# Bidirectional delta-net and attention encoder layer: small products of the block inversion issued in turn over different squares of the TensorE array

## Chip, cores, metric

One core of one Trainium2 chip. The metric is the device time of one execution in microseconds. An encoder layer runs on a prompt of 1024 tokens and a sample of 256 tokens.

## What is computed

A projection of the input feeds two groups of heads, a gated delta rule that runs forward and backward, and differential attention. Their outputs are projected, and a SwiGLU layer follows. The part that matters here is the delta rule. Each chunk of tokens needs the inverse of a unit triangular matrix, which the reference gets by a triangular solve:

```
decay = exp(where(incl, gc[..., :, None] - gc[..., None, :], -inf))
m = where(strict, einsum('bhnid,bhnjd->bhnij', kb, k) * decay, 0.0)
a_mat = m + eye(CHUNK)
rhs = concatenate([v * beta[..., None], kb * exp(gc)[..., None]], -1)
sol = triangular_solve(a_mat, rhs, left_side=True, lower=True, unit_diagonal=True)
u, w = sol[..., :DV], sol[..., DV:]
```

## The kernel before, in words

The kernel has phases. Phase A (`phase_a`) makes the dense projections on TensorE (line 172, tiles `dps`) and, between them, everything that the delta rule needs ahead of its scan: convolution and transposes, Gram products (line 430, `kq_ps`), decays, and the inverses. Attention scores (lines 839 and 840, `s_ps`), the scan with its loads `ld` (line 973), the output projection and the SwiGLU layer (lines 1281 and 1507) follow.

Five sets of eight 128x128 matrices per direction are inverted. VectorE inverts the 32x32 diagonal blocks (`invert_blocks`). They go out to HBM in plain and transposed form and come back into the tiles `UD` (`spread_blocks`: stores at lines 512 and 514, eight loads at line 517, issued by SP). `k.UD[0]`, which the listings call UD_772, holds the plain form; `k.UD[1]`, UD_773, the transposed one. Then `invert_levels` joins blocks on TensorE, in four stages with a `yield` between them; u counts the eight matrices and d the two directions:

- stage 1: 32 matmuls of 32x32 from `N` and UD_773 into one PSUM tile `inv_ps`, copied by VectorE to `Z`;
- stage 2: 48 matmuls of 32x32 from `Z` and `UD`, in six groups of eight, copied to `UD` by ScalarE and VectorE in turn;
- stage 3: per direction 8 matmuls of 64x64, each with its own `inv_ps`, copied to `Z` by ScalarE;
- stage 4: 16 matmuls of 64x64 in two groups, copied to `UD`, which is then stored for the scan (line 578).

The pool of `inv_ps` has one buffer. Every matmul reads 32 or 64 partitions (a group of rows of the array) and writes 32 or 64 (a group of columns); the pair is called a square here. The helper `pe` issues the eight matmuls of one group, all on one square:

```
for u in range(8):
    lhs, rhs = fn(u)
    nc.tensor.matmul(ps[rows, c0 + u * m:c0 + (u + 1) * m], lhsT=lhs, rhs=rhs, start=True, stop=True)
```

The stages stand in generators that `advance()` steps between pieces of the dense projection, and a scheduler then orders the instructions of each engine by its own estimate of when their inputs are there. So a change in one helper can move instructions on all queues.

Of the kernel before, what the change touches and what calls it, by code (L numbers as in the profile page):

```python
# [519 lines left out]
def diag(k, t, b, d=None):  # L520

    r = slice(32 * b, 32 * b + 32)
    return k.UD[t][r, :, r] if d is None else k.UD[t][r, 8 * d:8 * d + 8, r]


def invert_levels(k, si, vh, N, G):

    nc, V, A, PO = k.nc, k.nc.vector, k.nc.scalar, k.nc.gpsimd
    q = [slice(32 * b, 32 * b + 32) for b in range(4)]
    lo, up = slice(0, 64), slice(64, 128)  # L530
    UD = [[t[:, 8 * d:8 * d + 8] for t in k.UD] for d in range(2)]

    def pe(ps, rows, c0, m, fn):
        for u in range(8):
            lhs, rhs = fn(u)
            nc.tensor.matmul(ps[rows, c0 + u * m:c0 + (u + 1) * m], lhsT=lhs, rhs=rhs, start=True, stop=True)
        return ps[rows, c0:c0 + 8 * m].rearrange("p (u c) -> p u c", u=8)

    Z = k.gi.tile([P, 2, 8, 64], F32, tag="Z", name="Z")
    ps = k.pi.tile([P, 512], F32, tag="inv", name="inv_ps")  # L540
    for x, y in ((0, 1), (2, 3)):
        for d in range(2):
            pe(ps, q[y], 256 * d, 32, lambda u: (N[d][q[x], u, q[y]], diag(k, 1, x, d)[:, u]))
    for y in (1, 3):
        V.tensor_copy(Z[q[y], :, :, 0:32], ps[q[y], :].rearrange("p (d u c) -> p d u c", d=2, u=8))
    yield
    ps = k.pi.tile([P, 512], F32, tag="inv", name="inv_ps")
    out = []
    for d in range(2):
        U, D = UD[d]  # L550
        for x, y in ((0, 1), (2, 3)):
            if d == 0 or x == 2:
                r = pe(ps, q[x], 256 * d, 32, lambda u: (Z[q[y], d, u, 0:32], diag(k, 0, y, d)[:, u]))
                out.append((U[q[x], :, q[y]], r))
            if d == 1 or x == 0:
                r = pe(ps, q[y], 256 * d, 32, lambda u: (diag(k, 0, y, d)[:, u], Z[q[y], d, u, 0:32]))
                out.append((D[q[y], :, q[x]], r))
    for i, (o, r) in enumerate(out):
        (V.tensor_copy if i % 2 else A.copy)(o, r)
    yield  # L560
    for d in range(2):
        U, D = UD[d]
        ps = k.pi.tile([P, 512], F32, tag="inv", name="inv_ps")
        r = pe(ps, up, 0, 64, lambda u: (N[d][lo, u, up], D[lo, u, lo]))
        A.copy(Z[up, d], r)
    yield
    ps = k.pi.tile([P, 512], F32, tag="inv", name="inv_ps")
    U, D = UD[0]
    r0 = pe(ps, lo, 0, 64, lambda u: (Z[up, 0, u, :], U[up, u, up]))
    Ub, Db = UD[1]  # L570
    r1 = pe(ps, up, 0, 64, lambda u: (Ub[up, u, up], Z[up, 1, u, :]))
    A.copy(U[lo, :, up], r0)
    A.copy(Db[up, :, lo], r1)
    off = 4 * NT[si] + (vh * 8 if si == 1 else 0)
    V.tensor_tensor(out=Db, in0=Db, in1=G.nbeta[:, off:off + 8].unsqueeze(2).to_broadcast([P, 8, P]), op=ALU.mult)
    for g in range(2):
        for d, res in ((0, U), (1, Db)):
            nc.sync.dma_start(out=k.S.rec[si][vh][g][:, :, 6 * d, :], in_=res[:, 4 * g:4 * g + 4, :])
    yield
# [12 lines left out]
def phase_a(k):  # L592
    nc, tc = k.nc, k.tc
    with ExitStack() as es:
# [63 lines left out]
        def prep(si, vh, c3):  # L658
            N = []
            flag = Ctx()  # L660
            flag.done = False

            def front():
                yield from prep_front(k, si, vh, c3, k.G[si], N, flag, lambda: k.gp2 and len(blocks_) + len(levels) < 2)

            def invert():
                yield from invert_blocks(k, si, vh)

            def back():
                spread_blocks(k, si, vh)  # L670
                yield from invert_levels(k, si, vh, N, k.G[si])

            fronts.append(([front()], [invert(), back()]))
            return flag
# [989 lines left out]
```

## Time and profile before

| what | us |
|---|---|
| timed, median of 3 | 1756.84 |
| timed, lowest and highest | 1756.25 and 1760.42 |
| the profiled execution | 1751.05 |
| its span, first to last instruction | 1749.3 |

In the profile PE is TensorE's matmuls, PEld its weight loads, DVE VectorE, ACT ScalarE, POOL GpSimd, and SP the queue that issues most DMAs. An fp32 matmul appears as two weight loads and two matmul records, so the 32 matmuls of a stage are x64. Where a helper issues many matmuls all have the helper's line, 536 before and 538 in the changed kernel. The granted clock is 1.00 for 2.4 GHz and 0.50 for 1.2 GHz. Numbers in brackets behind a row are idle time of its engine ahead of it, and what ended that.

### The profile page before, as it was taken

To read this page: it belongs to the slowest core of one execution; us is meant where nothing else is said; L and a number is where in the kernel's file an instruction comes from. 1 tells how busy PE (TensorE), PEld (TensorE's weight loads), DVE (VectorE), ACT (ScalarE), POOL (GpSimd) and SP (SyncE) were. 2 spreads that over 40 slices of the span, in tenths; PEclk is the share of its full clock that TensorE was granted. 3 is DMA by queue.
4 is the path that set the end of the run, shared out by engine and by line. 5 is a ranking of instruction groups with operands and counts; after the bars stand their busy time and mean duration, and the time that the engine had idled before them with its cause. 6 is when DMAs were issued, how large, how long until landed. Compare 5 with 4: busy or idle time off the path is not lost.

```text
span 1749.3 us, 27337 instructions
## 1 busy us (share of the span) xinstructions
PE 1694.2 (97%) x10234; PEld 1471.2 (84%) x10234; DVE 1191.9 (68%) x2114; ACT 777.5 (44%) x1518; POOL 213.1 (12%) x197
## 2 busy tenths in 40 slices
PE   8999999999988999999999999999999999999998
PEld 8898888888867998788888888888888887888886
DVE  4635968878575589885676866556656665666696
ACT  4457486564337677775114322222222223543330
POOL 1000000000014445532330000000000000000011
PEclk9999999999988999999999999999999999999999
DMA  6234265676667996516521544333333524975541
GB/s 219 65 100 115 75 164 176 155 207 168 184 172 218 280 266 200 173 51 223 159 96 43 191 149 149 111 128 131 116 136 125 175 99 138 391 254 172 174 158 72
DMA packets 253554, 279.02 MB, mean 160 GB/s; under 512 B 47713, under 2 KB 198127, under 8 KB 252015
## 3 DMA queue, kind: packets, MB, share of 16 engines
q1 hardware_dynamic: 243519, 265.19, 48.5%
q10 hardware_dynamic: 9904, 12.10, 2.0%
q8 instruction: 80, 1.31, 0.3%
q14 instruction: 51, 0.42, 0.1%
HBM read 183.80 MB, written 93.43 MB: 158 GB/s over the span
## 4 chain that ended last, share of the span: by engine, by line
PE 54%; DMA 1%; ACT 1%; DVE 1%; issue 1%; POOLq 0%; POOL 0%; DVEq 0%; SPq 0%; ACTq 0%
PE dn_ps L1507 15%; PE gy_ps L1281 9%; PE gs_ps L1281 7%; PE gx_ps L1281 6%; PE gz_ps L1281 6%; PE om_ps L172 6%; PE gp_ps L1281 3%; DMA worw<-in_w_out_dram 1%; PE o_ps L879 1%; PE x_ps L1186 0%; ACT ap L843 0%; PE s_ps L839 0%; ACT woh L1166 0%; PE s_ps L840 0%; PE tt_ps L866 0%
## 5 line engine op out<-in xcount | busy, mean ns | idle before, releaser
L1297 ACT CAST sph<-wraw 128x512 fp32r<-128x512 f32 x92 | 57.0, 623 | 195.4 <-PE gy_ps L1281 124.4
L315 POOL TENSOR_TENSOR rs_r<-lva,mhalf 128x1 f32<-128x1 f32 x20 | 29.5, 1475 | 835.5 <-DVE lva L1143 817.1
L172 PE MATMUL dps<-xh,whi 128*128 128x512 f32 (+1 forms) x552 | 126.1, 363 | 0.0
L172 PE MATMUL dps<-xh,wlo 128*128 128x512 f32 (+1 forms) x552 | 124.5, 360 | 0.0
L172 PE MATMUL dps<-xl,whi 128*128 128x512 f32 (+1 forms) x552 | 123.4, 363 | 0.0
L1297 ACT CAST sph<-wsum 128x512 fp32r<-128x512 f32 x80 | 49.8, 622 | 156.6 <-PE gy_ps L1281 48.8
L1507 PE MATMUL dn_ps<-tth,ssh 128*128 128x512 f32 x280 | 108.9, 389 | 0.0
L1507 PE MATMUL dn_ps<-ttl,ssh 128*128 128x512 f32 x280 | 108.8, 389 | 0.0
L1507 PE MATMUL dn_ps<-tth,ssl 128*128 128x512 f32 x280 | 108.1, 389 | 0.0
L172 PEld LDWEIGHTS dps<-xh,wlo 128*128 128x128 f32 x552 | 94.8, 191 | 14.8
L172 PEld LDWEIGHTS dps<-xl,whi 128*128 128x128 f32 x552 | 94.2, 193 | 15.4
L172 PEld LDWEIGHTS dps<-xh,whi 128*128 128x128 f32 x552 | 94.5, 191 | 14.6
L841 DVE TENSOR_REDUCE ast<-s_ps 128x1 f32<-128x1024 f32 (+1 forms) x80 | 83.5, 1056 | 21.7 <-PE s_ps L840 19.6
L1298 DVE TENSOR_TENSOR spl<-wraw,sph 128x512 fp32r<-128x512 f32 x92 | 63.0, 687 | 48.2 <-PE gs_ps L1281 29.9
L334 DVE SCALAR_TENSOR_TENSOR c<-pad,cw,c 128x1024 f32<-128x1024 f32 (+1 forms) x96 | 82.1, 884 | 17.1 <-ACT c L332 16.6
L843 ACT ACTIVATE ap<-s_ps,ast 128x1024 f32<-128x1024 f32 (+1 forms) x80 | 80.0, 1001 | 29.4 <-DVE ast L841 29.1
L1298 DVE TENSOR_TENSOR spl<-wsum,sph 128x512 fp32r<-128x512 f32 x80 | 55.0, 688 | 46.6 <-issue 20.4
L1498 ACT CAST ssh<-sraw 128x640 fp32r<-128x640 f32 x77 | 56.0, 727 | 47.6 <-PE dn_ps L1507 34.3
L1499 DVE TENSOR_TENSOR ssl<-sraw,ssh 128x640 fp32r<-128x640 f32 x77 | 63.1, 820 | 16.8 <-ACT ssh L1498 13.1
L839 PE MATMUL s_ps<-akl,aq 128*128 128x512 f32 (+1 forms) x144 | 63.7, 444 | 7.7 <-ACT ap L843 7.6
L855 POOL TENSOR_TENSOR ap<-ap,ap 128x512 f32<-128x512 f32 (+2 forms) x60 | 63.0, 1069 | 64.6 <-ACT ap L852 31.6
L879 PE MATMUL o_ps<-av,tt 128*128 128x128 f32 x544 | 64.2, 275 | 0.0
(398 smaller groups left out, 4258.9 us busy)
## 6 DMA issues: line engine op xcount, KB each, us to landing
ld<-rec SPq DMA_DIRECT2D x160, 192.0 KB, 4.2
sraw<-hs SPq DMA_DIRECT2D x77, 320.0 KB, 4.3
wraw<-in_w_gate_up_dram SPq DMA_DIRECT2D x22, 1024.0 KB, 5.7
wraw<-in_w_in_dram SPq DMA_DIRECT2D x26, 512.0 KB, 4.5
wdraw<-in_w_down_dram SPq DMA_DIRECT2D x11, 1024.0 KB, 5.1
ws<-wdraw SPq DMA_DIRECT2D x11, 1024.0 KB, 3.9
traw<-ws SPq DMA_DIRECT2D x44, 256.0 KB, 4.5
araw<-dqk SPq DMA_DIRECT2D x40, 256.0 KB, 5.4
```

Of the source, the lines that this page charges most:

```text
L172: nc.tensor.matmul(out, lhsT=a(i), rhs=b(i), start=start and j == 0, stop=stop and j == len(seq) - 1)
L334: V.scalar_tensor_tensor(out=out, in0=pad[:, so + w:so + w + n], scalar=k.cw[:, w * 12 + ti:w * 12 + ti + 1], in1=out, op0=ALU.mult, op1=A ...
L839: nc.tensor.matmul(ps[:, o:o + w], lhsT=a.q[m][:, qs], rhs=a.kl[m][:, k0 + o:k0 + o + w], start=True, stop=False)
L841: V.tensor_reduce(out=st[:, m:m + 1], in_=ps, op=ALU.max, axis=AX.X, negate=True)
L843: A.activation(p, ps, AF.Exp, bias=st[:, m:m + 1], accum_out=a.s0[:, i:i + 1] if m == 0 else st[:, 2:3])
L855: nc.gpsimd.tensor_tensor(out=pr[0][:, c], in0=pr[0][:, c], in1=pr[1][:, c], op=ALU.add)
L879: nc.tensor.matmul(ps[:, j * P:(j + 1) * P], lhsT=tt[:, i, j * P:(j + 1) * P], rhs=a.v[:, v0 + i, :], start=i == 0, stop=i == NT[a.si] - 1)
L1281: m = nc.tensor.matmul(ps, lhsT=a(i), rhs=b(i), start=start and j == 0, stop=stop and j == len(seq) - 1, skip_group_check=again)
L1297: A.copy(hi, src)
L1298: V.tensor_tensor(out=lo, in0=src, in1=f32(hi), op=ALU.subtract)
L1499: V.tensor_tensor(out=lo, in0=src, in1=f32(hi), op=ALU.subtract)
L1507: nc.tensor.matmul(ps, lhsT=a[:, c], rhs=b, start=z == 0 and j == 0, stop=z == NPR - 1 and j == 2)
```

## The change

`pe` takes several groups at once and issues, for each u, one matmul of every group before it goes to the next u. Stage 1 is issued as two such calls (one for each direction, over two squares), stage 2 as one call over its six groups on four squares, stage 4 as one call over its two groups. Stage 3 has one group per call, as before. The list of the six groups of stage 2 is written out by a helper `product`, in an order in which neighbours use different squares where they can; which of the copies behind stage 2 ScalarE and VectorE take is given by that order.

```
-    def pe(ps, rows, c0, m, fn):
+    def pe(ps, *jobs):
         for u in range(8):
-            lhs, rhs = fn(u)
-            nc.tensor.matmul(ps[rows, c0 + u * m:c0 + (u + 1) * m], lhsT=lhs, rhs=rhs, start=True, stop=True)
-        return ps[rows, c0:c0 + 8 * m].rearrange("p (u c) -> p u c", u=8)
+            for rows, c0, m, fn in jobs:
+                lhs, rhs = fn(u)
+                nc.tensor.matmul(ps[rows, c0 + u * m:c0 + (u + 1) * m], lhsT=lhs, rhs=rhs, start=True, stop=True)
+        return [ps[rows, c0:c0 + 8 * m].rearrange("p (u c) -> p u c", u=8) for rows, c0, m, fn in jobs]
...
-    for x, y in ((0, 1), (2, 3)):
-        for d in range(2):
-            pe(ps, q[y], 256 * d, 32, lambda u: (N[d][q[x], u, q[y]], diag(k, 1, x, d)[:, u]))
+    for d in range(2):
+        pe(ps, *((q[y], 256 * d, 32, lambda u, x=x, y=y: (N[d][q[x], u, q[y]], diag(k, 1, x, d)[:, u])) for x, y in ((0, 1), (2, 3))))
...
+    def product(o, x, y, d, left):
+        outs.append(o)
+        if left:
+            jobs.append((q[y], 256 * d, 32, lambda u: (diag(k, 0, y, d)[:, u], Z[q[y], d, u, 0:32])))
+        else:
+            jobs.append((q[x], 256 * d, 32, lambda u: (Z[q[y], d, u, 0:32], diag(k, 0, y, d)[:, u])))
+    (Uf, Df), (Ub, Db) = UD
+    product(Uf[q[0], :, q[1]], 0, 1, 0, False)
+    product(Uf[q[2], :, q[3]], 2, 3, 0, False)
+    product(Df[q[1], :, q[0]], 0, 1, 0, True)
+    product(Db[q[3], :, q[2]], 2, 3, 1, True)
+    product(Db[q[1], :, q[0]], 0, 1, 1, True)
+    product(Ub[q[2], :, q[3]], 2, 3, 1, False)
+    out = list(zip(outs, pe(ps, *jobs)))
...
-    r0 = pe(ps, lo, 0, 64, lambda u: (Z[up, 0, u, :], U[up, u, up]))
-    r1 = pe(ps, up, 0, 64, lambda u: (Ub[up, u, up], Z[up, 1, u, :]))
+    r0, r1 = pe(ps, (lo, 0, 64, lambda u: (Z[up, 0, u, :], U[up, u, up])), (up, 0, 64, lambda u: (Ub[up, u, up], Z[up, 1, u, :])))
```

On TensorE, stages 1 and 2 of the first inversion stood like this before (a row with UD_773 and 32x32 is stage 1, rows with Z are stage 2):

```order
L536 MATMUL inv_ps<-UD_773,N 32x32 x32
L430 MATMUL kq_ps<-kqT 128x256 x4
L397 MATMUL t_ps<-identr,raw 128x128 x4
L172 MATMUL dps<-xh_153,whi 128x512 x5
L172 MATMUL dps<-xl_218,whi 128x512 x8
L536 MATMUL inv_ps<-UD_772,Z 32x32 x8
L536 MATMUL inv_ps<-Z,UD_772 32x32 x8
L536 MATMUL inv_ps<-UD_772,Z 32x32 x8
L536 MATMUL inv_ps<-Z,UD_772 32x32 x8
L536 MATMUL inv_ps<-UD_772,Z 32x32 x8
L536 MATMUL inv_ps<-Z,UD_772 32x32 x8
```

The same place in the changed kernel, cut behind the first rows of stage 2:

```order
L538 MATMUL inv_ps<-UD_773,N 32x32
L430 MATMUL kq_ps<-kqT 128x256 x3
L538 MATMUL inv_ps<-UD_773,N 32x32 x31
L430 MATMUL kq_ps<-kqT 128x256
L397 MATMUL t_ps<-identr,raw 128x128 x4
L172 MATMUL dps<-xh_153,whi 128x512 x5
L172 MATMUL dps<-xl_218,whi 128x512 x8
L172 MATMUL dps<-xh_217,wlo 128x512 x8
L172 MATMUL dps<-xh_217,whi 128x512
L538 MATMUL inv_ps<-UD_772,Z 32x32 x2
L538 MATMUL inv_ps<-Z,UD_772 32x32 x3
L538 MATMUL inv_ps<-UD_772,Z 32x32 x3
```

Stage 1 is parted into its first matmul and the other 31, with three Gram products between them, and stage 2 stands behind nine more dense matmuls and changes square after every matmul or two.

On SP, the DMAs between the last preparations of the second inversion's blocks and its loads, before (514 stores the transposed blocks, 517 loads them, 182 loads weights of the projection):

```order
L469 DMA Wb<-nblk_68 64x1024
L517 DMA UD_772<-ublk_70 32x16x32 x4
L514 DMA ublk_70<-itmp 64x1024
L469 DMA Wb<-nblk_68 64x1024
L359 DMA rec_66<-vn 512x1x128
L404 DMA e_f<-gc_58 128x512
L517 DMA UD_773<-ublk_70 32x16x32 x4
L182 DMA wraw<-in_w_in_dram 128x8x128
```

And in the changed kernel:

```order
L512 DMA ublk_70<-Ub 64x1024
L517 DMA UD_772<-ublk_70 32x16x32 x4
L514 DMA ublk_70<-itmp 64x1024
L182 DMA wraw<-in_w_in_dram 128x8x128
L517 DMA UD_773<-ublk_70 32x16x32 x4
```

The stores and loads of `Wb`, `vn` and `e_f` have gone ahead of this piece, and a weight load (182) stands between the store of the transposed blocks and their four loads.

On TensorE, the fifth inversion's stage 1 and the attention scores between it and stage 2, before:

```order
L839 MATMUL s_ps<-akl,aq 128x512
L840 MATMUL s_ps<-akh,aq 128x512
L536 MATMUL inv_ps<-UD_773,N 32x32 x32
L839 MATMUL s_ps<-akl,aq 128x512
L840 MATMUL s_ps<-akh,aq 128x512
L839 MATMUL s_ps<-akl,aq 128x512
L840 MATMUL s_ps<-akh,aq 128x512
L536 MATMUL inv_ps<-UD_772,Z 32x32 x8
```

And in the changed kernel, whose lines from the score matmuls on stand eight further down (847 and 848 for 839 and 840):

```order
L847 MATMUL s_ps<-akl,aq 128x512
L848 MATMUL s_ps<-akh,aq 128x512
L538 MATMUL inv_ps<-UD_773,N 32x32 x32
L847 MATMUL s_ps<-akl,aq 128x512
L848 MATMUL s_ps<-akh,aq 128x512
L847 MATMUL s_ps<-akl,aq 128x512
L848 MATMUL s_ps<-akh,aq 128x512
L847 MATMUL s_ps<-akl,aq 128x512
L848 MATMUL s_ps<-akh,aq 128x512
L847 MATMUL s_ps<-akl,aq 128x512
L848 MATMUL s_ps<-akh,aq 128x512
L538 MATMUL inv_ps<-UD_772,Z 32x32 x2
```

Eight score matmuls instead of four stand between the two stages; ahead of stage 1 there are now 16 score matmuls where there were eight.

## Rows read from the trace of the kernel before

**Rows 1.** The page: busy time, share of the span and count of TensorE and the others; TensorE's busy tenths in 40 slices of the span; its granted clock in the same slices.

```profile
PE 1694.2 (97%) x10234; PEld 1471.2 (84%) x10234; DVE 1191.9 (68%) x2114; ACT 777.5 (44%) x1518; POOL 213.1 (12%) x197
...
PE   8999999999988999999999999999999999999998
...
PEclk9999999999988999999999999999999999999999
```

**Rows 2.** All engines by windows. Columns: the stretch in us, its length, then busy us and count for PE, PEld, DVE, ACT and POOL, the granted clock, DMA share and GB/s.

```profile
234.60:238.00 3.40, 3.40 (x11) 2.58 (x10) 0.42 (x1) 1.56 (x6) 0.00 (x0) 0.50 0.80 246
238.00:323.00 85.00, 85.00 (x508) 73.42 (x507) 72.61 (x124) 64.99 (x147) 3.12 (x3) 1.00 0.68 182
323.00:326.80 3.80, 2.20 (x51) 1.67 (x50) 3.80 (x8) 0.00 (x0) 0.00 (x0) 0.99 0.85 199
326.80:333.60 6.80, 6.80 (x38) 5.67 (x35) 5.38 (x16) 5.16 (x9) 3.18 (x2) 0.50 0.40 127
...
398.50:401.90 3.40, 1.92 (x35) 1.41 (x35) 3.33 (x9) 0.56 (x2) 0.00 (x0) 0.99 0.83 151
401.90:408.70 6.80, 6.80 (x56) 6.06 (x54) 6.42 (x17) 4.63 (x12) 0.00 (x0) 0.50 0.62 186
...
510.60:514.50 3.90, 0.37 (x2) 0.00 (x0) 1.85 (x2) 0.00 (x0) 0.00 (x0) 1.00 0.90 272
514.50:535.00 20.50, 17.13 (x180) 13.54 (x180) 10.43 (x16) 12.14 (x18) 5.12 (x4) 0.50 0.50 106
...
600.00:1000.00 400.00, 386.92 (x2440) 341.44 (x2439) 307.66 (x587) 212.01 (x432) 132.27 (x117) 1.00 0.51 162
1000.00:1749.00 749.00, 738.54 (x3681) 628.34 (x3679) 485.12 (x800) 229.96 (x377) 14.23 (x10) 1.00 0.45 156
```

**Rows 3.** The same view for the instructions of line 536 alone. Columns: stretch, length, PE and PEld busy with counts, clock, DMA share, GB/s. In order: stage 1, stage 2, second half of stage 3, and stage 4 of the first inversion; stages 1, 2 and 4 of the fifth.

```profile
224.13:226.17 2.04, 2.03 (x64) 2.00 (x64) 1.00 1.03 324
231.51:234.16 2.65, 2.64 (x96) 2.61 (x96) 1.00 0.56 159
...
251.60:252.66 1.06, 1.06 (x16) 1.00 (x16) 1.00 1.02 183
259.63:261.45 1.82, 1.82 (x32) 1.76 (x32) 1.00 0.04 9
...
517.02:520.35 3.33, 3.33 (x64) 3.27 (x64) 0.50 0.81 183
522.36:526.67 4.31, 4.31 (x96) 4.26 (x96) 0.50 0.40 107
539.74:541.56 1.82, 1.82 (x32) 1.76 (x32) 1.00 0.01 5
```

**Rows 4.** Order of time on PE, the first inversion's stage 2 up to and behind the first change of group. Columns: start, length, then engine, line and form; inv_ps<-UD,Z and inv_ps<-Z,UD are the two kinds of groups.

```profile
231.52 0.59 PE L536 MATMUL inv_ps<-UD,Z 32*32 32x32 f32 x13
231.92 0.21 PE L536 MATMUL inv_ps<-Z,UD 32*32 32x32 f32 x1
231.95 0.19 PE L536 MATMUL inv_ps<-UD,Z 32*32 32x32 f32 x1
231.98 0.19 PE L536 MATMUL inv_ps<-Z,UD 32*32 32x32 f32 x1
231.98 0.19 PE L536 MATMUL inv_ps<-UD,Z 32*32 32x32 f32 x1
232.01 0.19 PE L536 MATMUL inv_ps<-Z,UD 32*32 32x32 f32 x1
232.01 0.19 PE L536 MATMUL inv_ps<-UD,Z 32*32 32x32 f32 x1
232.04 0.48 PE L536 MATMUL inv_ps<-Z,UD 32*32 32x32 f32 x10
```

**Rows 5.** The same view, the first inversion's stage 4.

```profile
259.63 0.97 PE L536 MATMUL inv_ps<-UD,Z 64*64 64x64 f32 x13
260.38 0.27 PE L536 MATMUL inv_ps<-Z,UD 64*64 64x64 f32 x1
260.44 0.22 PE L536 MATMUL inv_ps<-UD,Z 64*64 64x64 f32 x1
260.49 0.22 PE L536 MATMUL inv_ps<-Z,UD 64*64 64x64 f32 x1
```

**Rows 6.** Waits between 220 and 545 us: who waited for what, us in total, times, longest.

```profile
PE inv_ps L536 <- DMA UD<-ublk: 9.8, 5, 6.1
```

**Rows 7.** The waits of SP's queue in the same stretch.

```profile
SPq L182 <- DVE wlo L163: 28.1, 5, 17.5
...
SPq L973 <- PE inv_ps L536: 15.7, 1, 15.7
```

**Rows 8.** Order of time on PE: stage 1 of the second inversion (two rows) and of the third, and the first matmul of the scan.

```profile
324.90 1.19 PE L536 MATMUL inv_ps<-UD,N 32*32 32x32 f32 x32 [1.41 <-DMA UD<-ublk]
326.28 1.61 PE L536 MATMUL inv_ps<-UD,N 32*32 32x32 f32 x32 [0.19 <-DMA UD<-ublk]
...
400.94 2.83 PE L536 MATMUL inv_ps<-UD,N 32*32 32x32 f32 x64 [1.48 <-DMA UD<-ublk]
...
547.84 0.77 PE L1027 MATMUL vn_ps<-ld,ld 128*128 128x128 f32 x2 [3.66 <-DMA ld<-rec]
```

More of the change, by code (lines that the diff above doesn't have):

```diff
@@ L547, in invert_levels @@
     ps = k.pi.tile([P, 512], F32, tag="inv", name="inv_ps")
[L548 to L557, printed above, removed]
+    outs, jobs = [], []
+    def product(o, x, y, d, left):
[12 more added lines that the diff above has]
+    out = list(zip(outs, pe(ps, *jobs)))
     for i, (o, r) in enumerate(out):
@@ L563, in invert_levels @@
         ps = k.pi.tile([P, 512], F32, tag="inv", name="inv_ps")
-        r = pe(ps, up, 0, 64, lambda u: (N[d][lo, u, up], D[lo, u, lo]))
+        r, = pe(ps, (up, 0, 64, lambda u: (N[d][lo, u, up], D[lo, u, lo])))
         A.copy(Z[up, d], r)
```

## The prediction

> **What bounds the kernel now.** I read the page first: TensorE is busy for 97% of the span and VectorE for 68%, and TensorE's tenths stand at 9 nearly throughout [rows 1]. So the stretches with the inversions, from 220 to 545 us, were looked at next, by windows [rows 2]: from 238 to 323 us TensorE is busy for all 85.0 us. What shortens TensorE's work there shortens the run, as long as the next matmul in its queue is ready; and behind it TensorE remains nearly full (386.9 of 400 us, then 738.5 of 749 us), so time won early is not won again by a later wait. The exceptions in [rows 2] are short: 3.8 us with 2.2 us busy at 323, 3.4 with 1.9 at 398.5, and 3.9 with 0.4 at 510.6.
>
> Each inversion has four stages of small matmuls, and there are five inversions. [Rows 3] prices them. An fp32 matmul is two records (a stage of 32 is x64); I call a record a pass. Undisturbed, stage 1 takes 2.03 us (64 passes, 32 ns each), stage 2 takes 2.64 us (96 passes, 27.5 ns), each half of stage 3 takes 1.06 us (16 passes) and stage 4 takes 1.82 us (32 passes). That makes 8.6 us for one inversion.
>
> The decisive view is the order of time inside stage 2 [rows 4]. Its six groups of 16 passes use different squares of the array. Within a group a pass starts about every 31 ns (13 from 231.52 to 231.92). Where the group changes, the new group's first pass starts at 231.92, **ahead of** three passes of the old one (231.95, 231.98, 232.01), and the two then alternate: seven starts in 0.12 us. Each group keeps its own 31 ns. That is why six groups of 0.5 us take 2.64 us and not 3.0. Stage 4 shows the same for 64x64 squares: a pitch of about 60 ns in one square, then both squares at once [rows 5]. So the limit of a stage is its square, and two squares run side by side whenever the queue reaches the second one. The old order lets that happen for three or four passes per change of group.
>
> **The change, part by part.** No matmul, copy or DMA is added or removed; the order within a stage changes.
>
> Stage 1: two squares with 32 passes each, now alternating. Lower bound 32 x 31 ns = 1.0 us, upper bound the present 2.03 us. [Rows 4] show two squares at full rate, so I take 1.1 us: 0.9 us less.
>
> Stage 2: four squares; the fullest two have 32 passes, so 1.0 us is the lower bound. The trace never shows more than two squares at once; two at a time gives 96 x 15.6 ns = 1.5 us. I take 1.4 us, nearer the case that the rows show: 1.25 us less.
>
> Stage 3: one square at a time, with a single-buffered PSUM tile between its halves. Nothing.
>
> Stage 4: two squares with 16 passes each: 16 x 61 ns = 0.98 us at least, plus the drain; 1.1 us against 1.82: 0.7 us less.
>
> Sum: 2.85 us per inversion. For the four inversions among dense projections, where TensorE has other work to go on with, 4 x 2.85 = 11.4 us. The bounds are nothing and, with 1.0 + 1.6 + 0.8 = 3.4 us each, 13.6 us.
>
> Fifth inversion: the clock is granted at 0.50 from 514.5 to 535 us [rows 2], and stages 1, 2 and 4 take 3.33, 4.31 and 1.82 us [rows 3]. By the same shares that is about 1.2 + 2.0 + 0.7 = 3.9 us of TensorE work. It lies on a chain: SP's first load for the scan waits 15.7 us for these matmuls [rows 7], and TensorE then stands 3.66 us for that load [rows 8]. But the scheduler now puts 40 score matmuls ahead of its end where there were 36, and those wait for ScalarE and VectorE in turn. I take 2 us, between nothing and 4.
>
> **What the new order moves besides.** The build reorders the neighbours too. Stage 1 is now its first matmul, then three or four matmuls of other work in four of the five inversions, then the other 31. The second matmul needs another block of UD, so the wait for the second load moves forward by 31 matmuls; at 324.9 us it cost 0.19 us behind the first 32 passes, after 1.41 us for the first load [rows 8]. The matmuls put in between cover some of that.
> Five waits of stage 1 for these loads cost TensorE 9.8 us, 6.1 of them in the fifth inversion [rows 6]. For the second inversion 16 more 512-column and 5 more 256-column projections now stand ahead of stage 1, which hides its wait; but on SP a weight load (L182), which waits for VectorE, is put between the store of the transposed blocks and the UD_773 loads that stage 1 needs. Such weight loads wait 28.1 us in all, 17.5 at most [rows 7]. For the third inversion 28 fewer 512-column projections stand ahead, and the whole of TensorE arrives earlier, so its wait (1.48 us) can grow by several us. For the fourth, 33 more stand ahead, and its wait goes. I count these as zero, with a range from 3.7 us won (all waits but the fifth's) to 10 us lost (two waits of 3 to 4 us more, each with a spell of slow clock).
>
> The clock: it is granted at 0.50, that is 1.2 GHz, for 3.4 us right behind the first inversion's stage 2 and for twice 6.8 us behind a wait and a stage 1 [rows 2]. That is 17 us in which dense work is done at half the rate, some 8.5 us lost. Shorter stages let dense matmuls in sooner, which speaks for fewer such spells, but the waits that come ahead of two of them may stay or grow. From 0 to 8.5 us won; I take nothing, as a balance to the loads.
>
> Sum against the profiled execution: 1751.05 us (its span of 1749.3 and 1.75 us around it) - 11.4 - 2.0 = **1737.6 us**. That execution is 5.8 us below the median of the timed runs, 1756.84 us, which I expect to move by the same 13.4 us: **1743.4 us**.
>
> **The rivals.**
> Rival A: issue is the limit, not the square. The densest sustained pace in the trace is stage 2's 27.5 ns per pass. If TensorE's queue cannot feed passes faster, stage 1 falls only to 64 x 27.5 = 1.76 us, stage 2 not at all, stage 4 by its 0.7 us: 1.0 us x 5 = 5 us, 1752 us. For it: nothing in the trace sustains a faster pace. Against it: the seven starts in 0.12 us, and that the queue has run ahead by three passes again at every change of group. The Trainium skill (TensorE: Matmul & The Clock Gate, section "Wait — 56ns, not 53.3ns?") says that start-to-start never drops below about 25 ns however small the matmul; the pairs of starts at 231.98 and 232.01 lie closer than that, so as a floor for each pass the trace contradicts it, and as a sustained pace no run here decides; by it stage 2 would be an estimated 2.4 us.
>
> Rival B (no gain, or slower): the loads. TensorE reaches stage 1 of the second and third inversion before UD_773 has landed, because of the L182 ahead of the loads and of the earlier arrival. It decides from the point where two such waits grow by more than 3 us each and the clock falls to 0.50 behind both, as it did at 326.8 and 401.9 [rows 2]: 2 x (3.5 + 3.4) = 14 us against the 13.4 won: 1757 us, up to 1762. For it: four of the five stage 1 already wait. Against it: the same scheduler that moved the loads moved projections ahead of stage 1 in the second and fourth inversion.
>
> Rival C (slower): order is kept and every change of square costs. The first two passes of a new group are 0.06 us apart in stage 2, not 0.03 [rows 4], and 0.11 against 0.06 in stage 4 [rows 5]. If a square's passes may not overtake and each pair starts afresh, stage 2 is 48 x (53 + 31) ns = 4.0 us, 1.4 more, stage 1 0.7 more, stage 4 0.9 more: 3.0 us x 4 and some 4 for the fifth: 16 us slower, 1773 us. It would decide as soon as no pass starts ahead of an older one. Against it are 231.92 ahead of 231.95. The Trainium skill (same page, section "Step-by-step: what each phase is for") says that matmuls stay in program order and that only weight loads are pulled ahead; for matmuls of different squares the starts in [rows 4] contradict it.
>
> **Chances.** 0.3% of the median, 5.3 us, is about what a measurement of this kernel can tell from no change. The forecast (squares run side by side, loads about even) gets 0.72 and spans 1730 to 1751 us. Rival A gets 0.10, half of it beyond the 5.3 us. Rival B gets 0.13, of which 0.04 is over 0.3% slower. Rival C gets 0.03; 0.02 is left for a reordering that does harm later. Faster: 0.72 and 0.05 from A, 0.77; slower: 0.04 + 0.03 + 0.01, 0.08; the rest, 0.15, within. The range goes from 1729 us (all stages at their lower bounds and most of the slow clock gone) to 1756 us (A and the milder half of B).
>
> **What would show it.** In the new trace stage 2 should take 1.0 to 1.5 us for its 96 passes where they are not interrupted, stage 1's last 62 passes about 1.0 us, stage 4 about 1.1 us, each stage 3 half still 1.06. If stage 2 still takes 2.4 us or more, A holds; if it takes 4, C. If stages are short and the time is not, the waits of TensorE for UD<-ublk will have risen above 9.8 us, or the slow-clock spells between 220 and 545 us above 37 us. The forecast is wrong if stage 2 stays above 2 us or if those waits grow by more than 6 us.

## The result, and the profile after

The changed kernel takes 1765.2 us (median; 1762.05 to 1772.07), the kernel before 1756.25 us on the same chip (1753.73 to 1760.42): ratio 1.0055, 95% interval 1.0037 to 1.0072. It is 0.5% slower where 0.8% faster was forecast, and lies outside the range of 1729 to 1756 us. The profiled execution took 1762.96 us (span 1761.2).

The page of the changed kernel (TensorE's busy row, its tenths, its clock) answers to [rows 1]:

```profile
PE 1678.8 (95%) x10234; PEld 1452.8 (82%) x10234; DVE 1193.9 (68%) x2114; ACT 775.5 (44%) x1518; POOL 212.2 (12%) x197
...
PE   8999999899876999999999999999999999999998
...
PEclk9999999899987999999999999999999999999999
```

TensorE works 15.4 us less (1694.2 to 1678.8) in a span that is 12 us longer. So it idles more, and the tenths show where: 8, 7 and 6 in the slices from 440 to 570 us.

The windows of the small matmuls' line (now 538), answering to [rows 3]: columns as there; in order stage 1 of the first inversion without its first matmul, stage 2, the second half of stage 3 and stage 4 of the first inversion; stages 1, 2 and 4 of the fifth:

```profile
225.70:226.90 1.20, 1.17 (x62) 1.06 (x62) 1.00 1.02 332
232.87:234.10 1.23, 1.19 (x96) 1.10 (x96) 1.00 0.22 65
252.70:253.80 1.10, 1.10 (x16) 0.97 (x16) 1.00 1.06 202
260.60:261.75 1.15, 1.11 (x32) 1.01 (x32) 1.00 0.89 229
528.40:531.10 2.70, 2.18 (x64) 1.91 (x64) 0.50 0.53 90
534.40:535.75 1.35, 1.21 (x96) 1.09 (x96) 1.00 0.68 127
547.10:548.25 1.15, 1.11 (x32) 1.01 (x32) 1.00 0.00 0
```

Stage 1 falls from 2.03 to about 1.2 us, stage 2 from 2.64 to 1.19, stage 4 from 1.82 to 1.11; the half of stage 3 stays near 1.1. The order of time on TensorE at the start of stage 2 answers to [rows 4]:

```profile
232.91 0.22 PE L538 MATMUL inv_ps<-UD,Z 32*32 32x32 f32 x2
232.92 0.22 PE L538 MATMUL inv_ps<-Z,UD 32*32 32x32 f32 x2
232.96 0.20 PE L538 MATMUL inv_ps<-UD,Z 32*32 32x32 f32 x2
232.97 0.20 PE L538 MATMUL inv_ps<-Z,UD 32*32 32x32 f32 x2
232.99 0.20 PE L538 MATMUL inv_ps<-UD,Z 32*32 32x32 f32 x2
233.00 0.22 PE L538 MATMUL inv_ps<-Z,UD 32*32 32x32 f32 x2
```

In these first rows four passes start every 0.03 us: four squares at once, each at its old pace. Over the whole stage it is about three, 96 passes in 1.02 us from first start to last, because two of the four squares have twice as many passes as the others and set its length. The mechanism of the change works, and better than I took.

The waits of TensorE from 220 to 610 us (who waited for what, us in all, times, longest) answer to [rows 6], and the three worst places, in order of time, to [rows 8]:

```profile
PE inv_ps L538 <- DMA UD<-ublk: 13.7, 7, 7.9
PE s_ps L847 <- ACT ap L851: 10.2, 4, 5.9
```

```profile
339.28 0.31 PE L538 MATMUL inv_ps<-UD,N 32*32 32x32 f32 x2 [7.88 <-DMA UD<-ublk]
...
522.29 0.79 PE L847 MATMUL s_ps<-akl,aq 128*128 128x512 f32 x1 [5.91 <-ACT ap L851]
...
559.91 0.77 PE L1035 MATMUL vn_ps<-ld,ld 128*128 128x128 f32 x2 [8.10 <-DMA ld<-rec]
```

The first is stage 1 of the second inversion (1.41 us before), the last the scan's first matmul (547.84 us and 3.66 us before). The one between stands in the score matmuls ahead of the fifth inversion's stage 1, of which there are now eight more; all waits of score matmuls for ScalarE's `ap` come to 10.2 us, where the kernel before has 2.4. Around the first and the last the clock is at half, from 336.1 us, inside the first wait, and from 551.2 us, just ahead of the last, answering to [rows 2] (columns as there):

```profile
336.10:346.40 10.30, 6.78 (x78) 5.76 (x79) 4.39 (x16) 3.13 (x6) 2.34 (x1) 0.50 0.48 124
...
551.20:568.30 17.10, 8.50 (x33) 7.24 (x32) 4.77 (x5) 4.22 (x8) 3.16 (x3) 0.50 1.01 330
```

Why the second inversion is late: VectorE and SP's queue in order of time, changed kernel.

```profile
322.04 0.22 DVE L511 COPY Ub<-Ub 64x128 f32<-64x128 f32 x1
322.29 1.28 DVE L334 SCALAR_TENSOR_TENSOR c<-pad,cw,c 128x256 f32<-128x256 f32 x3
...
327.19 1.12 DVE L513 COPY itmp<-Ub 64x1024 f32<-64x1024 f32 x1
```

```profile
329.93 1.97 SPq L517 DMA_DIRECT2D UD<-ublk  x4
332.00 0.48 SPq L514 DMA_DIRECT2D ublk<-itmp  x1
332.52 0.59 SPq L182 DMA_DIRECT2D wraw<-in_w_in_dram  x1
334.96 2.06 SPq L517 DMA_DIRECT2D UD<-ublk  x4
```

Before, L511 stood at 311.3, L513 at 315.1, L514 at 316.9 and the last four loads from 321.0. Now VectorE has more convolution rows (L334) ahead of and between the two copies (29 in place of 19 since the first inversion's copy L511, then 8 in place of 6), and the loads that stage 1 needs go out 14 us later. The weight load L182, which I had blamed, takes 0.6 us.

Why the scan is late, first part: SP's queue in order of time, changed kernel, then the kernel before.

```profile
549.94 0.47 SPq L803 DMA_DIRECT2D araw<-dqk  x1
550.50 0.53 SPq L981 DMA_DIRECT2D ld<-rec  x1
551.15 1.23 SPq L586 DMA_DIRECT2D rec<-UD  x2
552.43 0.65 SPq L981 DMA_DIRECT2D ld<-rec  x1
...
554.80 3.34 SPq L981 DMA_DIRECT2D ld<-rec  x6
```

```profile
541.70 2.25 SPq L973 DMA_DIRECT2D ld<-rec  x5
544.05 1.24 SPq L578 DMA_DIRECT2D rec<-UD  x2
```

Five scan loads went out at once at 541.7; now an araw transfer stands ahead of them, waiting for VectorE's L814, and the four stores of UD stand between them. The waits of SP's queue from 545 us, answering to [rows 7], name the first:

```profile
SPq L803 <- DVE aq L814: 15.1, 1, 15.1
```

This is not the whole of it. The scan is 12.1 us later than before (559.91 and 547.84), and the fifth inversion's stage 4, behind whose matmuls the loads went out before [rows 7], is itself 7.4 us later (547.1 and 539.7 us). Experiment 3 below parts the two.

### The profile page after: what moved, and what is told of

Read it like the earlier page. It is cut to its first block, busy times and chain, and to the rows that moved or that the text cites. A ratio compares the mean times of both kernels' runs of the same rounds, so it can differ in the third digit from the quotient of the medians.

```text
span 1761.2 us, 27362 instructions
## 1 busy us (share of the span) xinstructions
PE 1678.8 (95%) x10234; PEld 1452.8 (82%) x10234; DVE 1193.9 (68%) x2114; ACT 775.5 (44%) x1518; POOL 212.2 (12%) x197
## 4 chain that ended last, share of the span: by engine, by line
PE 55%; ACT 1%; DVE 1%; issue 1%; DMA 0%; POOLq 0%; POOL 0%; DVEq 0%; SPq 0%
PE dn_ps L1515 15%; PE gy_ps L1289 9%; PE gs_ps L1289 7%; PE om_ps L172 6%; PE gx_ps L1289 6%; PE gz_ps L1289 6%; PE gp_ps L1289 2%; PE o_ps L887 1%; PE x_ps L1194 0%; PE tt_ps L874 0%; PE s_ps L847 0%; ACT ap L851 0%; PE s_ps L848 0%; DMA sraw<-hs 0%; DMA worw<-in_w_out_dram 0%
## 5 line engine op out<-in xcount | busy, mean ns | idle before, releaser
L334 DVE SCALAR_TENSOR_TENSOR c<-pad,cw,c 128x1024 f32<-128x1024 f32 (+1 forms) x96 | 81.9, 878 | 20.2 <-ACT c L332 19.8
```

The costliest lines, as they stand in the source:

```text
L334: V.scalar_tensor_tensor(out=out, in0=pad[:, so + w:so + w + n], scalar=k.cw[:, w * 12 + ti:w * 12 + ti + 1], in1=out, op0=ALU.mult, op1=A ...
```

## The experiments

Theory T: the turns win, and the scheduler's other order of the work around them loses more. Rival R: the turns themselves cost. Rival S: TensorE's won time is waited away at the loads of UD, whatever the order. To part them, the program is built more than once: one build gives the order of each engine's instructions, and the last build is held to an order by an edge from each instruction to the next one of its engine. The fences here give each edit in short. Which of the copies behind stage 2 go to ScalarE and which to VectorE belongs to the build and not to the order: it is as before in experiments 1, 5 to 10, 13 and 14, and as in the changed kernel in 2, 3, 4 and 12.

```diff
         with TileContext(...) as tc:
             hymba_layer(tc, *args)
+            if order is not None:
+                keep(tc, order)          # i behind the one ahead of it on its engine
...
+    was, now = build(turns=()), build(turns=(1, 2, 4))   # the orders of the two kernels
```

Ratios are to the kernel before, timed on the same chip in the same rounds; there it took 1758.5 to 1761.7 us.

**1. Turns, old order.** `build(turns=(1, 2, 4), order=was)`.

> The kernel before with the order of every engine's instructions held as it was, TensorE's loads, SP's transfers and all else; only the 96 small passes of stages 1, 2 and 4 inside their stages stand in turn, as in the changed kernel. Theory T (the turns win, the scheduler's other order of the surrounding work loses): TensorE's busy time falls by about 15 us as in the changed kernel (1694 to 1679) and nothing else moves, so about 1756.3 - 13 = 1743 us, between 1740 and 1748. Rival R (the turns themselves cost: what the array wins is lost to a wait on the products' results or to the clock, whatever the order around them): not under 1756 us, up to 1765. Rival S (the won time is lost again at the loads of UD, whatever the order, because the loads do not come earlier): 1750 to 1756 us, with the wait for UD<-ublk grown from 9.8 us by about what the stages won.

Measured: 1755.45 us, ratio 0.9969 (0.9955 to 0.9984). Faster, so R falls; but 5.5 us (0.31% of 1760), not 13, so T is half the story. A gain of 5.5 us is where S had it (nothing to 6 us), and the wait for UD<-ublk is longer, as S had it too (shown below). **This kernel is faster than both.**

**2. Groups, new order.** `build(turns=(), order=now)`.

> The changed kernel with its own order of every engine's instructions held; only the small passes inside their stages go back to one group after the other. Theory T: the new order without the gain of the turns, about 1765 + 13 = 1778 us (1772 to 1782), with TensorE busy about 1694 us and the first matmul of the recurrence still waiting some 8 us for ld<-rec. Rival R (the turns cost): 1756 to 1765 us. Rival S: about 1768 us, since the loads would hide most of the difference.

Measured: 1773.02 us, 1.0077 (1.0048 to 1.0106). The new order alone costs 0.77%, some 13.6 us. The changed kernel is 0.2% below that, so here too the turns win nothing like the 13 us of T (0.2% is within the two intervals). The scan's first matmul waits 8.4 us for ld<-rec here too. So the loss belongs to the order.

**A second profile of the kernel before.**

> The kernel before once more, for a second profile: every theory expects 1750 to 1766 us as in its timed runs. It shows how far two profiled executions of the same instructions differ: if by 5 us or more at the recurrence's start, differences of that size between single traces of two kernels prove nothing; TensorE's busy time should agree within 2 us, the waits for UD<-ublk within 4.

Its span is 1758.8 us, against 1749.3: the first profile of before was a short one. At the second inversion the same instructions now wait

```profile
330.00 3.43 PE L537 MATMUL inv_ps<-UD,N 32*32 32x32 f32 x64 [5.86 <-DMA UD<-ublk]
```

where they had waited 1.41 us. Single traces of two kernels differ by several us at one place for no reason of the code; what follows rests on timed ratios, or on busy times and intervals that repeat, and says where it has a single trace. From the first inversion's loads to the 41st score matmul, all engines (columns as [rows 2]): before, before again, and experiment 1.

```profile
222.40:550.40 328.00, 309.08 (x2434) 263.46 (x2433) 241.35 (x435) 185.61 (x404) 28.93 (x18) 0.93 0.63 173
```

```profile
221.90:554.60 332.70, 309.06 (x2433) 263.49 (x2432) 243.18 (x437) 186.36 (x408) 28.91 (x18) 0.93 0.64 170
```

```profile
223.60:550.60 327.00, 294.81 (x2433) 247.47 (x2432) 242.63 (x435) 185.27 (x404) 28.92 (x18) 0.93 0.64 173
```

The same work, and TensorE is busy 14.3 us less (309.1 to 294.8). But the stretch is only 1.0 or 5.7 us shorter: TensorE stands idle for 32.2 us in place of 18.9 or 23.6. The wait for UD<-ublk is 20.6 us, where the two profiles of before have 9.8 and 13.0:

```profile
PE inv_ps L537 <- DMA UD<-ublk: 20.6, 8, 6.1
```

**3 and 4. Parts of the new order mended.** In the changed kernel, SP's transfers behind the fifth inversion's loads (3), or VectorE's and SP's instructions up to the second inversion's loads (4), in the old order.

```diff
-    order = now
+    order = now, with SP's entries behind the last load of UD sorted as in was             # 3
+    order = now, with DVE's and SP's entries up to the 16th load of UD sorted as in was    # 4
```

> The changed kernel with SP's transfers behind the loads of the last inversion's blocks back in the order of the kernel before (five ld loads ahead of the transfer of araw and ahead of the stores of UD), all else as in the changed kernel. Theory T: the wait of 8.10 us of the recurrence's first matmul for ld<-rec falls to 2 to 4 us, ld<-rec is issued at about 542 us in place of 550.5, and the run is 8 to 10 us shorter than the changed kernel: 1755 to 1757 us. Rival (the recurrence is late because of ScalarE's and VectorE's rows, and SP's order only shows it): 1763 us or over.

> The changed kernel with VectorE's and SP's instructions up to the second inversion's loads of UD in the order of the kernel before (the copy of itmp ahead of the convolution's rows), all else as in the changed kernel. Theory T: TensorE's stand of 7.9 us for UD<-ublk falls to 1 to 3 us, the landmarks at 345 to 435 us stand about 5 us earlier. If that is kept to the end: 1757 to 1760 us. If the late tail takes it back (the araw transfer and VectorE's rows end when they end, whatever TensorE did before): 1763 to 1766 us, with the wait for ld<-rec grown beyond 8.1 us.

Measured: 1.0024 (1.0009 to 1.0038) and 1.0008 (0.9993 to 1.0023), where the changed kernel has 1.0055: 0.3% and 0.5% won, less than expected for 3. The traces show part of it given back. In 3 the scan starts 6.2 us sooner, with the fifth inversion's stage 4 where it was (546.5 us): so by these two traces SP's order made about half of the scan's delay. The chain then waits for ScalarE; in 4 stage 1 of the second inversion waits 0.84 us in place of 7.88, and the scan's first matmul longer:

```profile
553.73 0.77 PE L1038 MATMUL vn_ps<-ld,ld 128*128 128x128 f32 x2 [2.76 <-DMA ld<-rec]
...
581.80 2.07 PE L1047 MATMUL ds_ps<-vn,ld 128*128 128x128 f32 x8 [3.65 <-ACT vn L1040]
```

```profile
331.54 0.24 PE L537 MATMUL inv_ps<-UD,N 32*32 32x32 f32 x2 [0.84 <-DMA UD<-ublk]
...
554.63 0.76 PE L1038 MATMUL vn_ps<-ld,ld 128*128 128x128 f32 x2 [9.91 <-DMA ld<-rec]
```

**12. Both at once.**

> The changed kernel with both mendings at once: VectorE's and SP's instructions up to the second inversion's loads, and SP's behind the fifth inversion's loads, in the order of the kernel before. Alone they gave 1.0024 (the tail) and 1.0008 (the second inversion) where the changed kernel has 1.0055. If these two places hold most of what the new order costs and their effects add: 0.997 to 0.9985, close to the first experiment's 0.9969. If the one hides behind the other (the tail ends when ScalarE's and VectorE's rows end, whatever SP does): 1.000 to 1.002, and the rest of the loss lies in the order of ScalarE and VectorE in the tail.

Measured: 0.9995 (0.9976 to 1.0014), between the two expectations. The two places hold about two thirds of what the new order costs (1.0055 to 0.9995, towards 0.9969, each known to 0.15 to 0.2%). The rest was not placed. One place left over shows in the trace: the score matmuls ahead of the fifth inversion still wait 4.0 us for ScalarE's `ap` (5.9 in the changed kernel; in 1 none of them waits there).

**5 and 6. Old order first, then new; and the reverse.** Cut at the first load of UD for the fifth inversion, passes in turn.

```diff
+    head = names of was (5) or now (6) up to the 33rd load of UD
+    order = head + [those of the other order that are not in head]
```

> Small passes in turn; every engine in the order of the kernel before up to the loads of UD for the fifth inversion (about 512 us), from there in the order of the changed kernel. With the first experiment (all in the old order, ratio 0.9969 to the kernel before) as foot: if the tail's order costs what the trace of the changed kernel showed there (ld<-rec 8.1 us and its half clock, the landmarks +13.5 us at 557 us and +9.5 later), about 1.0025 to 1.004, that is 1764 to 1767 us where the kernel before has 1760. If the tail's order costs nothing by itself and only passed on the delay of the second inversion: 0.996 to 0.998.

> The other half: the order of the changed kernel up to the loads of UD for the fifth inversion, from there that of the kernel before. If the tail alone decides: as the first experiment, 0.996 to 0.998. If the second inversion's late loads (7.9 us) are carried to the end: about 1.000 to 1.002. If both halves are needed for the loss (a late middle meets a tail that can't take it up): between 0.998 and 1.000 here, and in the other half too.

Measured: 0.9999 (0.9982 to 1.0016) and 1.0005 (0.9987 to 1.0023). Against experiment 1, the new tail costs 0.30% (5.3 us) and the new middle 0.36% (6.3 us), each to some 0.2%, together most of the 0.86% between the changed kernel and experiment 1. Neither half alone is the culprit. (6 has a wait of its own at the seam: 12.9 us for UD<-ublk at the fifth inversion.)

**7. The mirror image: more TensorE work, old order, groups.**

```diff
             nc.tensor.matmul(ps[...], lhsT=lhs, rhs=rhs, start=True, stop=True)
+            if twice:                       # stage 2 alone
+                nc.tensor.matmul(ps[...], lhsT=lhs, rhs=rhs, start=True, stop=True)
```

> The kernel before with its order held, groups one after another, and each pass of stage 2 issued twice into the same place: 96 more passes for each of five inversions, 2.5 us each by the stage's own length before, 12.7 us of TensorE in all. If TensorE is the bound in this stretch (as the prediction had it): +12 to +13 us, ratio 1.007. If VectorE's chain and the loads of UD are, and TensorE's time there is mostly waited away (rival S): +4 to +6 us, ratio 1.002 to 1.0035, and the wait for UD<-ublk falls under 9.8 us.

Measured: 1782.72 us, 1.0123 (1.0096 to 1.0150), 21 us more. The price was wrong: stage 2 grew by 3.6 to 5.1 us, 23.3 us over five inversions, not 12.7, as parts of it ran at half clock. Of those 23.3 us the run shows 21. (TensorE's busy time in the whole run grew by more, 29 to 31 us, the granted clock falling from 0.983 or 0.984 to 0.975 on average.) So adding TensorE time costs most of it, while removing 14.3 us won 5.5. S, as I put it, is refuted in this direction: TensorE and what feeds it are in balance here, and TensorE made longer shows almost in full.

**8. The stores of ublk and loads of UD issued by GpSimd,** else as 1.

```diff
-    nc.sync.dma_start(out=..., in_=...)      # the ten of spread_blocks
+    nc.gpsimd.dma_start(out=..., in_=...)
```

> The first experiment (passes in turn, old order) with the two stores of ublk and the eight loads of UD issued by GpSimd in place of SP, at the same places of the order. If it is SP's queue, in which these transfers stand behind others' waits, that makes the loads late: the wait for UD<-ublk falls from 20.6 us to about 15 and the run gets 3 to 5 us shorter than the first experiment (ratio 0.994). If they wait for VectorE's copies and for UD to come free: no gain, 0.997, or slower where GpSimd takes longer to issue them.

Measured: 0.9999 (0.9982 to 1.0016), slower than 1, and the wait for UD<-ublk is 31.9 us. The gain expected if SP's queue were at fault (0.994) did not come.

**9 and 10. Earlier copies and stores,** with turns and with groups.

```diff
+    order = was, with L513 right behind L511, L512 and L514 right behind L513,
+            and the loads of UD0 that stood ahead of L514 behind it
```

> The first experiment (old order held, passes in turn) with one thing earlier: VectorE's copy of Ub to itmp stands directly behind the copy in Ub, SP's two stores of ublk directly behind these, and the loads of UD0 that stood ahead of the second store behind it. By the traces that takes 3.7 us from the way to the first inversion's loads, 5 to 6 us from the second's, about 2 from the third's and fifth's. If the time that the turns win is lost at these loads (the wait for UD<-ublk of 20.6 us): the wait falls to 10 to 14 us and the run gets 4 to 8 us shorter than the first experiment, ratio 0.992 to 0.995. If the wait is only passed on (to N, to the recurrence's ld<-rec, to ScalarE): 0.996 to 0.998.

> The same early copy and stores with the passes in groups, as in the kernel before. Its wait for UD<-ublk was 9.8 us in all, 6.1 of it at the fifth inversion, where little is won. If the turns and the early stores help each other: 0.999 to 1.000 here, that is no gain of its own, and more than 6 us between this run and the one with the turns. If the early stores are worth the same with and without the turns: 0.995 to 0.997 here, with 5 us between the two.

Measured: 1.0008 (0.9994 to 1.0023) and 1.0024 (1.0008 to 1.0040): worse by 0.4% and 0.2% than without. SP's queue of 9 shows why:

```profile
313.39 0.48 SPq L514 DMA_DIRECT2D ublk<-itmp  x1
...
325.41 2.22 SPq L517 DMA_DIRECT2D UD<-ublk  x4
```

The store L514 goes out 6 us sooner than in 1 (319.60), yet the loads of UD1, which stage 1 needs, go out 2 us later (323.49 in 1): I had moved the stores ahead of other transfers, but left those loads behind all of them. The wait for UD<-ublk rises to 25.2 us. This edit did not test what it was meant to test.

**13 and 14. Less work for VectorE,** with turns and with groups, old order. Two of the convolution's four later taps are done on 16 columns only, so these kernels leave part of the convolution out.

```diff
         for w in range(1, 5):
-            V.scalar_tensor_tensor(out=out, in0=pad[:, so + w:so + w + n], ...)
+            m = 16 if w > 2 else n
+            V.scalar_tensor_tensor(out=out[:, :m], in0=pad[:, so + w:so + w + m], ...)
```

> The first experiment (old order held, passes in turn) with VectorE's last two of the four taps of the convolution done on 16 columns in place of 1024 or 256 (this leaves part of the convolution out): the 65 rows of L334 between 212 and 507 us took 42.4 us, so about 20 us of VectorE's work go from there. If VectorE's chain sets the pace there, the copies L511 move together, TensorE's wait for UD<-ublk falls from 20.6 us, and the run is 10 to 16 us shorter than the kernel before (ratio 0.991 to 0.994). If the turns lose their time elsewhere: as the run without the turns, less 5 us.

> The same lighter convolution with the passes in groups, as in the kernel before. TensorE was busy there for 309 of 328 us, so VectorE's lost work can win at most the waits of about 10 us for UD<-ublk: ratio 0.997 to 1.000. If VectorE's chain is why the turns won so little, the two runs lie 9 to 14 us apart (the turns' full worth); if the turns lose their time elsewhere, about 5 us as before.

Measured: 0.9906 (0.9891 to 0.9921) and 0.9960 (0.9945 to 0.9975), 1743.77 and 1753.76 us. With less on VectorE the turns are worth 0.54%, some 9.5 us, in place of 5.5; the lighter VectorE alone wins 7 us. That is what the first cause wanted, by little: 9 us or more were named for it, and 14 alone won more than the 0.997 expected. By the intervals the 9.5 us are known to 3.7 us, and the step from 0.31% to 0.54% is not clear of noise by itself. The scan's first matmul points the same way: in order 1, 14 and 13.

```profile
548.08 0.76 PE L1038 MATMUL vn_ps<-ld,ld 128*128 128x128 f32 x2 [1.91 <-DMA ld<-rec]
```

```profile
548.23 0.77 PE L1039 MATMUL vn_ps<-ld,ld 128*128 128x128 f32 x2 [4.25 <-DMA ld<-rec]
```

```profile
533.95 0.77 PE L1039 MATMUL vn_ps<-ld,ld 128*128 128x128 f32 x2 [2.57 <-DMA ld<-rec]
```

It stood at 547.84 and 552.09 us in the two profiles of before. The turns alone, or the lighter VectorE alone, do not move it out of that; both together bring it 14 us sooner, as much as TensorE has less to do. (These are single traces, and that of 14 is of the longest of its six timed runs, 1757.92 us, so some us of the 14 may be chance.) The wait for UD<-ublk is 14.9 us in 13, against 11.9 in 14: with the lighter VectorE the turns lengthen it by 3 us, where it was 7.6 to 10.8.

The row that shows the pace is the copy L511 (L512 in 13 and 14), once for each inversion: the first and last start stand behind the durations. In order: before, before again, 1, the changed kernel, 7, 14, 13.

```profile
L511 DVE COPY Ub<-Ub x5: 223/223/1333, 211.4 to 506.7; 64x128 f32<-64x128 f32 x5
```

```profile
L511 DVE COPY Ub<-Ub x5: 222/224/1357, 213.0 to 511.1; 64x128 f32<-64x128 f32 x5
```

```profile
L511 DVE COPY Ub<-Ub x5: 221/223/2239, 212.7 to 509.2; 64x128 f32<-64x128 f32 x5
```

```profile
L511 DVE COPY Ub<-Ub x5: 221/223/224, 212.7 to 516.2; 64x128 f32<-64x128 f32 x5
```

```profile
L511 DVE COPY Ub<-Ub x5: 222/223/1872, 211.2 to 529.5; 64x128 f32<-64x128 f32 x5
```

```profile
L512 DVE COPY Ub<-Ub x5: 222/223/1628, 208.2 to 502.1; 64x128 f32<-64x128 f32 x5
```

```profile
L512 DVE COPY Ub<-Ub x5: 222/222/1228, 208.5 to 496.0; 64x128 f32<-64x128 f32 x5
```

From first to last: 295.3 and 298.1 us before, 296.5 with the turns. So 14 us less of TensorE's work did not bring VectorE's fifth block any sooner. VectorE itself is busy for only 242.6 of the 327.0 us above: the limit is a chain that runs through it, with waits in it, and not a full engine. With the new order it is 303.5; with stage 2 doubled 318.3. With less on VectorE it is 293.9 with groups and 287.5 with turns: now the turns do shorten it, by 6.4 us (the two profiles of before differ by 2.8).

## Why the prediction was wrong, step by step

- **The stages' price** was right in kind and low in size. Taken: 2.85 us per inversion; shown: 0.85 + 1.45 + 0.71 = 3.0 us, and 15.4 us of TensorE's busy time over the run. For stage 2 the starts keep to the bound of 1.0 us (four squares at once): they lie within 1.02 us, and with the last pass's own length the stage takes 1.19 us, not the 1.4 taken.
- **Rivals A and C** fall with the same rows: stage 2 does 96 passes within 1.02 us, first start to last, or 10.7 ns per pass.
- **"4 x 2.85 = 11.4 us"**, with TensorE having "other work to go on with", is the first step that failed. With the old order held, 5.5 us were won (1), though TensorE had 14.3 us less to do. I read 85.0 of 85.0 us busy and concluded that TensorE alone was the limit. VectorE's copies L511 come no sooner for it, so TensorE reaches stage 1 earlier and waits: 20.6 us for UD, where it had waited 9.8 or 13.0. The busy rows could not show this second limit right under the first. The fifth inversion's 2 us stand under the same mistake, since its blocks came no sooner. In the changed kernel a wait came on top that I had named without a price: the score matmuls now put ahead of stage 1 stand 5.9 us for ScalarE. (By the shares that I used, the fifth's stage 1 would have been 1.5 us shorter, not 1.2; that changes nothing.)
- **"I count these as zero"** (what the new order moves besides) is the step that turned the sign. The range went from 3.7 us won to 10 lost; the new order cost 13.6 us with groups (2) and 15 with turns (the changed kernel against 1), beyond either bound.
- **Rival B** was the right kind of case, at 0.13, and too narrowly put. The second inversion's loads were late, but by VectorE's convolution rows, as its trace has it, not by L182. The third, which I feared for, had no such wait. And the tail, where araw and the stores of UD came ahead of the scan's loads, I had read for ScalarE's and VectorE's waits alone, not for SP's queue: 0.3% by experiment 3, which puts back that queue alone, and as much by 5. For such later harm I had left 0.02.
- **The sign that I named** did not come: the waits for UD<-ublk grew by 3.9 us (9.8 to 13.7), not by more than 6. I had watched one wait; those of the score matmuls for ScalarE (7.8 us more) and of the scan for ld<-rec (4.4 us more) grew more than it did.
- **The clock** term of zero held in the net: 0.984 before, 0.983 in the second profile of before, 0.982 after. The spells moved with the waits; none was shown to be a cause of its own.
- **The median** was to move as the profile does. The profiled execution of before was a short one: its second profile is 9.5 us longer.

What stays open: a third of the new order's cost was not placed beyond "middle" and "tail". That VectorE's work limits what the turns win is supported by 13 and 14, by a timed step that is not clear of noise and by single traces that agree with it; which of its chain's links (its own rows, the loads it waits for, the matmuls that feed it) weighs most was not separated.

## What to carry to other kernels

Where an automatic scheduler orders the program, price a local change in two parts, the change itself and the new order of everything around it, and part them by holding one build to the order of the other: here the local change won 0.3% and its side effect cost 0.8%. An engine that is busy all the time may have a second limit directly beneath it; look at when the engine that feeds it delivers (one row per round, as L511 here) before you count a shorter stage as won time. And before you move a transfer up in a queue, move those that depend on it as well.

## What the runs showed of the hardware

Matmuls of four different squares of the array ran at once: 96 passes of 32x32 squares started within 1.02 us, 10.7 ns from start to start over all, which is the time of the 32 passes of the two fullest squares at 31 to 32 ns each. Two squares of 32x32 gave 62 passes in 1.00 us, 16 ns from start to start. I had counted on two at once. Doubling each pass into the same place kept the pace within a square, and the stage then ran partly at half clock (0.70 granted on average over the first inversion's 7.5 us), so that 96 more passes cost up to 5.1 us in place of 2.5.
